# One piece of a dense product moved across two pieces of an inverse, in an order written by hand

## The chip, the core and the metric

The kernel runs on one core of a Trainium2 chip. The metric is the time of one execution on the device in microseconds (us), the median of several runs. A core has five engines, each with an instruction queue of its own that it works through in order: TensorE (PE in the profile; its loading of weights is PEld), VectorE (DVE), ScalarE (ACT), GpSimd (POOL) and SyncE (SP), which here issues the DMA transfers. An engine whose next instruction waits for a semaphore waits with all that stands behind it.

## The reference

One layer of a streaming encoder, on a sequence of 4096 tokens with 1024 features. One projection feeds four mixers of 256 features each, whose outputs are joined and projected back; a gated embedding is added and the result is normed:

```python
z = x @ w_in[i]
y_a = rwkv7_mix(rw_in, ...) * jax.nn.silu(rw_g)
y_b = pool_mix(pl_u, ...) * jax.nn.silu(pl_g)
y_c = mlstm_mix(ml_qk, ...) * jax.nn.silu(ml_g)
y_d = retention_mix(rt_q, ...) * jax.nn.silu(rt_g)
ple = jax.nn.sigmoid(x @ ple_gate[i]) * (p[i] @ ple_w[i])
x = _layer_norm(DEEPNORM_ALPHA * x + mixed @ w_out[i] + ple, ln_g[i], ln_b[i], LN_EPS)
```

The change lies in the first mixer. Per head (4 heads of 64) it carries a 64 x 64 state through the tokens, decayed, corrected by a rank-one term and read by r:

```python
def step(state, inp):
    w_t, r_t, k_t, v_t, kk_t, ab_t = inp
    sa = jnp.einsum('bhvk,bhk->bhv', state, -kk_t)
    state = (state * w_t[:, :, None, :] + sa[..., None] * ab_t[:, :, None, :]
             + v_t[..., None] * k_t[:, :, None, :])
    return state, jnp.einsum('bhvk,bhk->bhv', state, r_t)
```

## The kernel before, in words

The mixers run one after the other: pooling, retention, mLSTM, then the RWKV mixer, then the output stage. The RWKV mixer takes the sequence in 16 blocks of 256 tokens, each of four chunks of 64. Within a chunk the recurrence is solved in closed form, which needs the inverse of a triangular 64 x 64 matrix for each head and chunk (8 at a time for half a block).

The work on a block is cut into pieces, generator functions that are advanced by an order written by hand, `ORDER`. Pass i (of 18) takes the dense projections and the scores of block i, the inverse's last steps of block i - 1 and the chain over the chunks of block i - 2; in the order, `v.0` is a piece of block i, `pu.1` of block i - 1, `C` a third of a chunk of the chain. Passes 0 to 2 have orders of their own; passes 3 to 17 use `ORDER`, and a piece whose block is past the last is left out. A number behind a slash says how many steps of a piece are made. The pieces that matter here:

- `la`, `k`, `r`, `g`, `v`: dense projections (lines 158 to 160). A step is one of the eight parts of the sum over features, six matmuls of 128 x 256. After the last step the result is mixed with the token before (L1366, L1369 on ACT, L1370, L1373 on DVE, zf L1349 on POOL).
- `s0`, `s1` (L416, L417): four transposes on PE into a PSUM tile st, which DVE copies, scaled, to ST.
- `p0`, `p1` (L262 as gp, L437): sixteen score matmuls into two PSUM tiles gp, from which eight DVE instructions write g.
- `bn` (L406): a small product for the bonus term, copied by ACT.
- `inv` (L492, L496): two DMAs nd write the triangular parts of g to DRAM, four DMAs nt bring them back in another layout. `iv` (L505, L514, L530 on DVE, L532, L535 on SP) inverts 16 x 16 blocks and sends them back as X.
- `pt` (Z by a DVE transpose at L546, PE), `px` (PE, L571 on DVE): the first two products that join the blocks. `pu` (Z by a DVE transpose of X at L580, PE, copied to T by ACT at L588) and `py` (PE, L601): the last two.
- `C`: ry on PE reads the state S, ACT copies it (R, L636), sa on PE (SAV, L643), then ds on PE, S on DVE (L660), ry again and Y on ACT (L666). After the fourth chunk the output Y is normed on DVE (bsr L718, mvr L720, rsr L722, a power on POOL at L723, Y at L732 and L733), scaled (L680, L681), joined with the bonus on POOL (L677, L685) and multiplied by the gate (L686).

Tiles named st, gp, bn, vt and l share two PSUM buffers in turn: `p1`'s first gp tile takes the one that `bn` had, its second the one of `s1`.

PE's order is kept as the pieces are called. On the other engines a scheduler in the build step, with a timeline of its own, decides the order within what the data allow; the chain and the steps of the inverse are marked as urgent (`soon`). What it has decided is fixed in the program.

Of the kernel before, what the change touches and what calls it, by code (L numbers as in the profile page):

```python
# [26 lines left out]
MM = 2  # L27
WK = 2
DS = "sd"
ORDER = "C la.0 C k.0/2 C k.0 C r.0/2 C l.0 r.0/3 C n.0 r.0/4 C vt.1 r.0 m.0 C g.0/4 C g.0 v.0/2 C s0.0 v.0/1 pt.1 C p0.0 v.0/2 px.1 C bn.0 v.0/1 s1.0 v.0/2 pu.1 v.0/1 p1.0 v.0 py.1 inv.0 iv.0"  # L30

START = "v#0/3 l#0 v#0 n#0 m#0 la#1 k#1/4 bn#0 s0#0 p0#0 k#1/2 s1#0 p1#0 inv#0 k#1 r#1/2 l#1 r#1 n#1 vt#0 iv#0 m#1 g#1 v#1 bn#1 s0#1 p0#1 s1#1 p1#1 pt#0 la#2 px#0 k#2/3 pu#0 inv#1 k#2 py#0 iv#1"

# [13 lines left out]
class Trunk:  # L47
# [148 lines left out]
    def _rwkv_out(self, es):  # L196
# [493 lines left out]
        for i in range(self.NB + 2):  # L690
            gens = {}
            for w in ("" if i == 1 else START if i == 0 else THIRD if i == 2 else ORDER).split():
                if w == "C":
# [1102 lines left out]
```

## Time and profile before

| | |
|---|---|
| median of 3 runs | 2755.69 us (2754.13 to 2758.62) |
| profiled execution | 2756.33 us, of which the span from the first to the last instruction is 2754.5 us |
| mean granted TensorE clock | 0.984 of full speed |
| busy: PE, PEld | 96%, 87% of the span |
| busy: DVE, ACT, POOL | 78%, 40%, 41% |
| RWKV mixer, passes 3 to 16 | from about 1316 to 1966 us |

Times in the rows are microseconds from the start of the span. An engine's busy time counts its instructions' own spans; matmuls are pipelined, and a matmul that waits behind another in the array counts as busy too. "Idle before" an instruction is time in which its engine had nothing running, with the releaser that ended it.

### The profile page before, as it was taken

How to read it: one execution, taken by the hardware profiler on the slowest of the kernel's cores; microseconds unless marked ns; L12 is line 12 of the kernel's file. 1: busy time of each engine (PE TensorE's matmuls, PEld its weight loads, DVE VectorE, ACT ScalarE, POOL GpSimd, SP SyncE). 2: the span in 40 equal slices, each digit the busy share in tenths (PEclk: the TensorE clock that was granted, in tenths of full speed). 3: DMA queues.
4: the chain of work that ended last, by engine and by line, in shares of the span. 5: the costliest groups of instructions: out<-in, count | busy, mean ns of one | idle time of the engine just before them, and what ended most of it. 6: DMA issues, size and time to landing. Idle time of an engine off the chain costs nothing.

```text
span 2754.5 us, 57727 instructions
## 1 busy us (share of the span) xinstructions
PE 2653.0 (96%) x21940; PEld 2382.7 (87%) x21940; DVE 2142.6 (78%) x5241; ACT 1111.2 (40%) x2700; POOL 1142.9 (41%) x1302
## 2 busy tenths in 40 slices
PE   8999999998999999989999999999989999899996
PEld 8998888878899999988999999998988888778885
DVE  6767888886887777777888888888564666789997
ACT  4323222334666666653444444445222333422221
POOL 4664555554433434431323333324243111266665
PEclk9999999999999999999999999999999999999998
DMA  5453222223311112231111111113366444734431
GB/s 170 146 174 113 59 61 66 66 69 95 99 55 58 55 55 65 74 107 34 53 39 51 39 51 39 51 40 110 117 197 220 135 140 145 237 123 156 157 138 69
DMA packets 251909, 270.66 MB, mean 98 GB/s; under 512 B 69616, under 2 KB 175344, under 8 KB 251632
## 3 DMA queue, kind: packets, MB, share of 16 engines
q1 hardware_dynamic: 251632, 266.98, 31.0%
q8 instruction: 172, 2.82, 0.4%
q14 instruction: 105, 0.86, 0.1%
HBM read 203.40 MB, written 63.50 MB: 97 GB/s over the span
## 4 chain that ended last, share of the span: by engine, by line
PE 40%; DVE 16%; DMA 7%; issue 4%; POOL 3%; ACT 2%; SPq 1%; POOLq 0%; DVEq 0%; ACTq 0%
PE ry L262 2%; DVE ro L1688 2%; PE zqk L150 2%; PE zqk L151 2%; PE zqk L149 2%; DVE nt L505 1%; DVE ro L1667 1%; DVE ro L1670 1%; PE zg L158 1%; DMA nd<-g 1%; POOL ro L1671 1%; PE zg L159 1%; PE zg L160 1%; DVE so L1662 1%; PE num L1265 1%
## 5 line engine op out<-in xcount | busy, mean ns | idle before, releaser
L1446 ACT CAST Ah<-xr 128x512 fp32r<-128x512 f32 x189 | 117.0, 620 | 280.7 <-PE zrb L1482 55.3
L1447 DVE TENSOR_TENSOR Al<-xr,Ah 128x512 fp32r<-128x512 f32 x135 | 95.6, 710 | 80.6 <-ACT Ah L1446 77.2
L150 PE MATMUL zqk<-xl,wh_w_ml 128*128 128x256 f32 x512 | 150.6, 294 | 0.8 <-DVE xl L1126 0.8
L149 PE MATMUL zqk<-xh,wh_w_ml 128*128 128x256 f32 x512 | 149.8, 293 | 1.5 <-ACT xh L1125 1.2
L88 ACT CAST xh<-rawx 128x512 fp32r<-128x512 f32 x148 | 91.5, 619 | 146.4 <-DMA rawx<-in_xT 65.9
L151 PE MATMUL zqk<-xh,wl_w_ml 128*128 128x256 f32 x512 | 148.5, 290 | 0.0
L89 DVE TENSOR_TENSOR xl<-rawx,xh 128x512 fp32r<-128x512 f32 x148 | 116.0, 784 | 28.5 <-ACT xh L88 27.5
L677 POOL TENSOR_TENSOR SAV<-SAV,bon 64x256 f32<-64x256 f32 x64 | 42.9, 671 | 227.2 <-PE ry L262 226.1
L1447 POOL TENSOR_TENSOR Al<-xr,Ah 128x512 fp32r<-128x512 f32 x54 | 71.0, 1314 | 139.7 <-ACT Ah L1446 75.3
L1671 POOL TENSOR_TENSOR ro<-ro,ln_b 128x512 f32<-128x512 f32 x64 | 100.7, 1593 | 53.9 <-DVE ro L1670 53.9
L912 POOL TENSOR_TENSOR rot<-rot,sw 128x256 f32<-128x256 f32 x64 | 69.2, 1082 | 95.4 <-DVE sw L911 89.5
L149 PEld LDWEIGHTS zqk<-xh,wh_w_ml 128*128 128x128 f32 x512 | 99.1, 194 | 3.2 <-ACT xh L1125 1.5
L150 PEld LDWEIGHTS zqk<-xl,wh_w_ml 128*128 128x128 f32 x512 | 99.4, 194 | 2.9 <-DVE xl L1126 1.0
L151 PEld LDWEIGHTS zqk<-xh,wl_w_ml 128*128 128x128 f32 x512 | 99.3, 194 | 0.8
L1466 POOL TENSOR_TENSOR xr<-xr,xr 128x512 f32<-128x512 f32 x27 | 35.6, 1317 | 143.0 <-DVE xr L1463 132.7
L660 DVE SCALAR_TENSOR_TENSOR S<-ds,eC,Se 64x64 f32<-64x64 f32 x256 | 72.4, 283 | 22.0 <-PE ds L262 17.0
L1237 DVE SCALAR_TENSOR_TENSOR xc<-zc,c_convw,xc 128x256 f32<-128x256 f32 x192 | 83.3, 485 | 0.4
L437 DVE SCALAR_TENSOR_TENSOR g<-gp,rc,c_rmask 128x128 f32<-128x128 f32 x256 | 69.0, 341 | 18.3 <-PE gp L262 17.2
L149 PE MATMUL zu<-xh,wh_w_pl 128*128 128x256 f32 x256 | 74.8, 292 | 6.1 <-ACT wh_w_pl L88 6.1
L657 POOL TENSOR_TENSOR Se<-S,eC 64x128 f32<-64x128 f32 x128 | 59.2, 463 | 48.8 <-DVE S L660 44.0
L150 PE MATMUL zu<-xl,wh_w_pl 128*128 128x256 f32 x256 | 73.8, 288 | 3.9 <-DVE xl L89 3.9
L1446 ACT CAST Aho<-s 128x512 fp32r<-128x512 f32 x48 | 29.7, 621 | 115.3 <-PE zob L1482 52.4
(1130 smaller groups left out, 10570.2 us busy)
## 6 DMA issues: line engine op xcount, KB each, us to landing
rawx<-in_xT SPq DMA_DIRECT2D x148, 256.0 KB, 3.2
xr<-in_xT SPq DMA_DIRECT2D x108, 256.0 KB, 2.9
mr<-in_xT SPq DMA_DIRECT2D x64, 256.0 KB, 3.1
rp<-in_x SPq DMA_DIRECT2D x64, 256.0 KB, 3.0
s<-rp SPq DMA_DIRECT2D x64, 256.0 KB, 2.7
yo<-y SPq DMA_DIRECT2D x16, 1024.0 KB, 4.9
ro<-s SPq DMA_DIRECT2D x16, 1024.0 KB, 5.0
out<-ro SPq DMA_DIRECT2D x32, 512.0 KB, 2.6
```

The lines of the kernel that those rows point to most:

```text
L88: nc.scalar.copy(out=hi, in_=raw)
L89: eng.tensor_tensor(out=lo, in0=raw, in1=hi.bitcast(F32), op=ALU.subtract)
L149: nc.tensor.matmul(out, lh(k), rh(k), start=(k == 0 and (apart or i == 0)), stop=False, skip_group_check=True)
L150: nc.tensor.matmul(out, lh(k), rl(k), start=False, stop=False, skip_group_check=True)
L151: nc.tensor.matmul(out, ll(k), rh(k), start=False, stop=(k == nk - 1), skip_group_check=True)
L437: V.scalar_tensor_tensor(out=g1[cc][:, hh, p, e], in0=gp[hh][:, p, e], scalar=rc[:, cc, e, i:i + 1], in1=msk[:, 64 * e:64 * e + P], op0=AL ...
L660: V.scalar_tensor_tensor(out=Sn[hv, p, hv], in0=ds[hv, p], scalar=eC[hv, p, c:c + 1], in1=Se[hv, p], op0=ALU.mult, op1=ALU.add)
L912: Q.tensor_tensor(out=r3, in0=r3, in1=sw, op=ALU.add)
L1237: V.scalar_tensor_tensor(out=xc[:, t], in0=zc[t // 2][:, t % 2, j:j + TB], scalar=cw[:, t, j:j + 1], in1=xc[:, t], op0=ALU.mult, op1=ALU.add)
L1446: self.nc.scalar.copy(out=hi, in_=src)
L1447: eng.tensor_tensor(out=lo, in0=src, in1=hi.bitcast(F32), op=ALU.subtract)
L1671: Q.tensor_tensor(out=rg, in0=rg, in1=ln["ln_b", g], op=ALU.add)
```

## The change

Only the text of `ORDER` is changed, at its end:

```diff
-ORDER = "... px.1 C bn.0 v.0/1 s1.0 v.0/2 pu.1 v.0/1 p1.0 v.0 py.1 inv.0 iv.0"
+ORDER = "... px.1 C bn.0 v.0/2 s1.0 pu.1 v.0 p1.0 py.1 inv.0 iv.0"
```

Five steps of `v` come before `bn` in both. Before, one more step stands ahead of the transposes s1, and the last two between them and pu (the later mentions of `v` find it finished). Now two steps stand ahead of s1, pu follows s1 directly, and the last step of `v` stands between pu and the scores of p1.

On PE, at the end of pass 8 (z8v is the dense product of `v`, st_1 the transposes of s1, pu the step of the inverse, gp_1 the scores of p1; of the six matmuls of a step some stand outside the piece shown):

```order
-L416 MATMUL st_1_20766<-c_ident,BK_20454 128x128 x4
 L158 MATMUL z8v<-xh_6_20172,wh_w_rw_14595 128x256
 L159 MATMUL z8v<-xl_6_20171,wh_w_rw_14595 128x256
...
 L160 MATMUL z8v<-xh_6_20172,wl_w_rw_14594 128x256
+L416 MATMUL st_1_20772<-c_ident,BK_20454 128x128 x4
+L262 MATMUL pu_20780<-Z_1_20778,g_0_19733 32x32 x8
+L262 MATMUL pu_20780<-Z_1_20778,g_1_19734 32x32 x8
 L158 MATMUL z8v<-xh_6_20172,wh_w_rw_14595 128x256
...
-L262 MATMUL pu_20793<-Z_1_20791,g_0_19733 32x32 x8
-L262 MATMUL pu_20793<-Z_1_20791,g_1_19734 32x32 x8
 L262 MATMUL gp_1_0_20813<-AR_1_20456,BK_20454 128x128
```

The transposes stand one step of six matmuls later, pu one step earlier, and a step of `v` is between pu and the scores.

On DVE, the same place of the program in the kernel before (Z_1 is what pu reads, ST_1 the copy of st_1, xl_6 and xl_0 parts of coming inputs, Y the chain's output, g_1 the masked scores):

```order
L580 STREAM_TRANSPOSE Z_1_20791<-X_20145 128x512
L718 BN_STATS bsr_20718<-Y_20148 128x6 x2
L720 BN_AGGR mvr_20719<-bsr_20718 128x2 x2
L417 TENSOR_TENSOR ST_1_20472<-st_1_20766,rc_14870 128x512
L89 TENSOR_TENSOR xl_6_20911<-rawx_6_20913,xh_6_20912 128x512
...
L722 TENSOR_SCALAR rsr_20736<-mvr_20719 128x8
L732 TENSOR_TENSOR Y_20148<-Y_20148,mvr_20719 128x512
L89 TENSOR_TENSOR xl_0_21633<-rawx_0_21635,xh_0_21634 128x512
...
L1373 TENSOR_TENSOR v_20784<-v_20784,zf_20177 128x2
L437 SCALAR_TENSOR_TENSOR g_1_20474<-gp_1_0_20813,rc_14870,c_rmask 128x128 x4
L437 SCALAR_TENSOR_TENSOR g_1_20474<-gp_1_1_20814,rc_14870,c_rmask 128x128 x4
L733 TENSOR_TENSOR Y_20148<-Y_20148,rsr_20736 128x512
```

and in the changed kernel:

```order
L580 STREAM_TRANSPOSE Z_1_20778<-X_20145 128x512
L718 BN_STATS bsr_20718<-Y_20148 128x6 x2
L89 TENSOR_TENSOR xl_6_20911<-rawx_6_20913,xh_6_20912 128x512
L720 BN_AGGR mvr_20719<-bsr_20718 128x2 x2
L417 TENSOR_TENSOR ST_1_20472<-st_1_20772,rc_14870 128x512
L722 TENSOR_SCALAR rsr_20736<-mvr_20719 128x8
L732 TENSOR_TENSOR Y_20148<-Y_20148,mvr_20719 128x512
...
L437 SCALAR_TENSOR_TENSOR g_1_20474<-gp_1_0_20813,rc_14870,c_rmask 128x128
...
L1373 TENSOR_TENSOR v_20806<-v_20806,zf_20177 128x2
L733 TENSOR_TENSOR Y_20148<-Y_20148,rsr_20736 128x512
L437 SCALAR_TENSOR_TENSOR g_1_20474<-gp_1_0_20813,rc_14870,c_rmask 128x128 x3
L437 SCALAR_TENSOR_TENSOR g_1_20474<-gp_1_1_20814,rc_14870,c_rmask 128x128 x4
```

ST_1 now stands behind xl_6 and a second pair of mvr, and L733 before seven of the eight g. Passes 3 to 6 and 8 to 13 are moved alike. A little later, where the inverse of the block begins, one instruction changes sides in these passes:

```order
 L309 TENSOR_TENSOR lal_18103<-la_17985,lah_18102 64x256
+L686 SCALAR_TENSOR_TENSOR Y_17188<-Y_17188,sg_16084 128x512
 L505 TENSOR_TENSOR nt_17894<-nt_17894,xs_14868 64x4
-L686 SCALAR_TENSOR_TENSOR Y_17188<-Y_17188,sg_16084 128x512
 L514 TENSOR_REDUCE xs_14868<-nt_17894 64x4
```

The gate product of Y stands before the inverse's first product instead of behind it. In pass 7 the scheduler has set another order on DVE, here from Z_1 on in the changed kernel:

```order
L580 STREAM_TRANSPOSE Z_1_20038<-X_19405 128x512
L718 BN_STATS bsr_19978<-Y_19408 128x6 x4
L720 BN_AGGR mvr_19979<-bsr_19978 128x2 x4
L722 TENSOR_SCALAR rsr_19996<-mvr_19979 128x8
L732 TENSOR_TENSOR Y_19408<-Y_19408,mvr_19979 128x512
L89 TENSOR_TENSOR xl_6_20171<-rawx_6_20173,xh_6_20172 128x512
L733 TENSOR_TENSOR Y_19408<-Y_19408,rsr_19996 128x512
L680 TENSOR_TENSOR Y_19408<-Y_19408,c_rw_ln_w 128x512
L417 TENSOR_TENSOR ST_1_19732<-st_1_20032,rc_14871 128x512
L681 TENSOR_TENSOR Y_19408<-Y_19408,c_rw_ln_b 128x512
```

In the kernel before, pass 7 has the same order as pass 8; here ST_1 stands behind L732, L733 and L680.

## Rows read from the trace of the kernel before

**Rows 1.** The page, busy time of each engine

```profile
PE 2653.0 (96%) x21940; PEld 2382.7 (87%) x21940; DVE 2142.6 (78%) x5241; ACT 1111.2 (40%) x2700; POOL 1142.9 (41%) x1302
```

**Rows 2.** Timeline of PE, pu: start, length, engine, line, out<-in, count [idle before]

```profile
1543.21 0.69 PE L262 MATMUL pu<-Z,g 32*32 32x32 f32 x32
...
1587.92 0.69 PE L262 MATMUL pu<-Z,g 32*32 32x32 f32 x32
...
1861.76 0.69 PE L262 MATMUL pu<-Z,g 32*32 32x32 f32 x32
```

**Rows 3.** Timeline of PE, the chain's third ry, passes 8 and 9

```profile
1566.67 0.62 PE L262 MATMUL ry<-S,AR 128*128 128x128 f32 x4
...
1611.81 1.10 PE L262 MATMUL ry<-S,AR 128*128 128x128 f32 x4 [0.26 <-DVE S L660]
```

**Rows 4.** Timeline of DVE, the start of the inverse after pass 8

```profile
1601.42 0.16 DVE L505 TENSOR_TENSOR nt<-nt,xs 64x4 f32<-64x4 f32 x1 [1.22 <-DMA nt<-nd]
1601.51 0.68 DVE L686 SCALAR_TENSOR_TENSOR Y<-Y,sg 128x512 f32<-128x512 f32 x1
1602.11 0.15 DVE L514 TENSOR_REDUCE xs<-nt 64x4 f32<-64x4 f32 x1
```

**Rows 5.** Timeline of SP, issues of nd and nt after passes 7 and 8

```profile
1548.85 1.26 SPq L492 DMA_DIRECT2D nd<-g  x2
1551.87 1.81 SPq L496 DMA_DIRECT2D nt<-nd  x4
...
1593.55 1.26 SPq L492 DMA_DIRECT2D nd<-g  x2
1598.17 1.81 SPq L496 DMA_DIRECT2D nt<-nd  x4
```

**Rows 6.** Timeline of PE, two neighbouring dense matmuls of pass 8

```profile
1587.59 0.28 PE L159 MATMUL z8v<-xl,wh_w_rw 128*128 128x256 f32 x1
1587.71 0.28 PE L160 MATMUL z8v<-xh,wl_w_rw 128*128 128x256 f32 x1
```

**Rows 7.** Timeline of DVE, from Z to g in pass 8

```profile
1587.06 0.69 DVE L580 STREAM_TRANSPOSE Z<-X 128x512 f32<-128x512 f32 x1
...
1588.17 0.69 DVE L417 TENSOR_TENSOR ST<-st,rc 128x512 f32<-128x512 f32 x1
1588.77 0.68 DVE L89 TENSOR_TENSOR xl<-rawx,xh 128x512 fp32r<-128x512 f32 x1
1589.37 0.24 DVE L720 BATCH_NORM_AGGREGATE mvr<-bsr 128x2 f32<-128x6 f32 x2
1589.53 0.45 DVE L1370 SCALAR_TENSOR_TENSOR v<-z8v,c_prm,v 128x255 f32<-128x255 f32 x1
1589.90 0.16 DVE L722 TENSOR_SCALAR rsr<-mvr 128x8 f32<-128x8 f32 x1
...
1591.63 2.15 DVE L437 SCALAR_TENSOR_TENSOR g<-gp,rc,c_rmask 128x128 f32<-128x128 f32 x8
```

**Rows 8.** Timeline of PE, the scores p1 of pass 8 and p0 of pass 9

```profile
1588.55 1.52 PE L262 MATMUL gp<-AR,BK 64*128 64x128 f32 x16
...
1626.14 1.16 PE L262 MATMUL gp<-AR,BK 64*128 64x128 f32 x16
```

**Rows 9.** Timeline of POOL and DVE, the power and who waits for it

```profile
334.10 2.62 POOL L723 TENSOR_TENSOR rst<-rst,pw 128x8 f32<-128x8 f32 x1
336.75 1.77 DVE L733 TENSOR_TENSOR Yt<-Yt,rst 128x512 f32<-128x512 f32 x1 [0.22 <-POOL rst L723]
...
1545.43 2.01 POOL L723 TENSOR_TENSOR rsr<-rsr,pw 128x8 f32<-128x8 f32 x1 [1.60 <-DVE rsr L722]
...
1590.13 2.63 POOL L723 TENSOR_TENSOR rsr<-rsr,pw 128x8 f32<-128x8 f32 x1 [1.59 <-DVE rsr L722]
```

**Rows 10.** PE in pass 15, then stretches: busy PE, PEld, DVE, ACT, POOL, granted clock, DMA

```profile
1884.09 1.03 PE L262 MATMUL n<-ones,sq 128*64 128x2 f32 x16 [1.37 <-ACT sq L340]
...
1881.00:1885.00 4.00, 2.51 (x40) 2.15 (x38) 4.00 (x9) 3.63 (x9) 1.94 (x2) 1.00 0.57 182
1885.30:1888.70 3.40, 3.40 (x18) 3.40 (x18) 3.29 (x11) 1.26 (x2) 1.26 (x4) 0.50 0.30 77
```

More of the change, by code (lines that the diff above doesn't have):

```diff
@@ L29 @@
 DS = "sd"
-ORDER = "C la.0 C k.0/2 C k.0 C r.0/2 C l.0 r.0/3 C n.0 r.0/4 C vt.1 r.0 m.0 C g.0/4 C g.0 v.0/2 C s0.0 v.0/1 pt.1 C p0.0 v.0/2 px.1 C bn.0 v.0/1 s1.0 v.0/2 pu.1 v.0/1 p1.0 v.0 py.1 inv.0 iv.0"
+ORDER = "C la.0 C k.0/2 C k.0 C r.0/2 C l.0 r.0/3 C n.0 r.0/4 C vt.1 r.0 m.0 C g.0/4 C g.0 v.0/2 C s0.0 v.0/1 pt.1 C p0.0 v.0/2 px.1 C bn.0 v.0/2 s1.0 pu.1 v.0 p1.0 py.1 inv.0 iv.0"
 START = "v#0/3 l#0 v#0 n#0 m#0 la#1 k#1/4 bn#0 s0#0 p0#0 k#1/2 s1#0 p1#0 inv#0 k#1 r#1/2 l#1 r#1 n#1 vt#0 iv#0 m#1 g#1 v#1 bn#1 s0#1 p0#1 s1#1 p1#1 pt#0 la#2 px#0 k#2/3 pu#0 inv#1 k#2 py#0 iv#1"
```

## The prediction

> **What bounds the kernel now.** The page's summary comes first: TensorE (PE) is busy 96% of the span [rows 1]. Taken alone that says that PE is the bound and that every wait added to PE is paid in full. The timeline of PE says it more finely. The second product of the inverse (pu) stands once in every pass, so its starts give the pace: from pass 8 to pass 14 it is (1861.76 - 1587.92) / 6 = 45.64 us, while pass 7 takes 1587.92 - 1543.21 = 44.71 us, 0.93 less [rows 2]. I compared the instructions of the two group by group: PE takes the same time for all of them, to 0.1 us, except at one place. There the step of the recurrence (ry, reading the state S) follows the dense matmuls without a pause in the short pass; in the normal one PE idles 0.26 us for DVE's S (L660), and the four matmuls then take 1.10 us instead of 0.62 [rows 3]: with the dense pipeline running empty before them, from start to start the 0.9 us. So about 0.9 us of PE's "busy" in each normal pass is waiting, and the pace is set by a second loop: VectorE's (DVE's) masked scores g of p1, their transfer to DRAM (nd) and back (nt), the row sums of the inverse (L505, L514, L530) on DVE, then S on DVE, then PE. The list of waits confirms its DMA part: DVE waits for nt in 11 of the passes, 1.22 us in pass 8 [rows 4]. In the short pass the second nd issue to the first nt issue takes 1551.87 - 1548.85 = 3.0 us, in a normal one 1598.17 - 1593.55 = 4.6 us [rows 5]. PE alone would do a pass in 44.7; the loop through DVE and DMA makes it 45.6. A change is worth what it does to the later of these two.
>
> **The change part by part.** It exists in 13 passes (3 to 15; in 16 and 17 the pieces v, s1 and p1 have no block left). No instruction is added or removed; the order fences show what moves. I work on pass 8 and then count.
>
> *PE, pu earlier.* Six dense matmuls, 0.12 us apart [rows 6], leave the place before pu: 0.72 us. In before pu starts at 1587.92 just behind them; without them it could at 1587.20. But pu reads Z, which DVE ends only at 1587.06 + 0.69 = 1587.75 [rows 7], and what DVE does before Z is not moved. So PE now waits some 0.55 us for Z, and starts pu hardly earlier (0.1 us) with 0.7 us of dense work still to do. In before, this piece of v was what covered Z.
>
> *PE, the second scores.* The scores gp of p1 need the PSUM buffer that the transposes st hold until DVE has copied them (ST, L417): before, gp takes 1.52 us here and 1.16 us at the first scores, where nothing is waited for, so 0.36 us is already that wait [rows 8]. On DVE, ST now stands behind xl_6 and two of the mvr: it moves by 1589.53 - 1588.77 = 0.76 us [rows 7]. gp's release moves with it, from 1588.86 to 1589.62, and the moved dense piece (1587.8 + 0.6 for pu + 0.8 = 1589.2) hides beneath. PE leaves this place 0.76 us later than before. PE's own pace becomes 44.71 + 0.76 = 45.47 us, still below 45.64: in a normal pass this alone costs nothing, since the 0.9 us wait for S shrinks by as much. Where that cover is gone (pass 7) it costs in full.
>
> *DVE, the scores g.* Y's second factor (L733) stood behind g and now stands before seven of its eight instructions. All else ahead of g is the same set, so DVE comes to L733 at g's old start 1591.63 plus one g (2.15 / 8 = 0.27), 1591.9. L733 reads the power that GpSimd (POOL) forms: in pass 8 it starts 0.23 us after rsr's start and takes 2.63 us; in pass 7 2.01 us [rows 9]. rsr moves to 1588.17 + 0.76 + 0.60 = 1589.53; the small zf on POOL may stand in front, so the power starts at about 1589.9 and ends at 1591.9 or 1592.5. DVE waits 0 or 0.6 us for it, L733 takes 0.60 (start to start, as xl does, 1589.37 - 1588.77 [rows 7]), and g ends 0.6 or 1.2 us later. nd and nt follow g, so nt lands that much later; DVE was waiting for it already.
>
> *DVE, the gate product.* L686 stood inside the inverse, behind its first L505, and now stands before it, in the time in which DVE waits for nt. The chain from nt to S loses it: 1602.11 - 1601.51 = 0.60 us [rows 4]. This is the change's one gain on the loop. Net on S: 0.6 - 0.6 = 0, with hand-overs say +0.1, or 1.2 - 0.6 = +0.6, say +0.7. Of the ten normal passes (3 to 6 and 8 to 13) five show the short power and five the long: 10 x 0.4 = 4.0 us, with 0 and 7 as bounds (all short, all long).
>
> Whether POOL's span may be trusted decides half of this. The row: in the retention stage the power starts at 334.10 and ends, by its 2.62 us, at 336.72; DVE, idle and waiting for it, starts at 336.75 [rows 9]. The Trainium skill (Perfetto Trace Analysis, Per-instruction lifecycle) tells readers to treat a GpSimd span in a profile as unreliable and to go by the spacing of instructions. By that rule the long powers need not be longer, and the term would be 10 x 0.1 = 1 us, the whole sum 7.5 instead of 10.5. Here the spacing agrees with the span, so I keep 4.0.
>
> *Pass 7.* There the new order on DVE is another: Z, all eight small statistics, rsr, Y, xl_6, L733, L680 and only then ST. With pass 8's durations: Z starts 0.27 earlier (1586.79), rsr is due at 1588.3, the power (2.01) ends at 1590.6, then L733 and L680 at 0.7 each, so ST starts at 1592.0 instead of 1588.17. gp, and all PE work behind it, moves by 3.8 us, and pass 7 is the one without a wait for S to take it up: +3.8 (with a long power +4.4). During such a wait the granted clock may fall: in pass 15, shortly after PE had idled 1.37 us for sq, the granted clock of 1885.3 to 1888.7 is 0.50, the lower of the two levels, 1.2 GHz, and 1.00 before [rows 10]. At half clock 3.4 us of dense work loses 1.7 us: +1.7, bounds 0 and two such stretches, 3.4.
>
> *Passes 14 and 15.* Gate weights and the first products of the last stage are mixed in, and DVE has hardly a pause. g ends 0.6 to 1.8 us later, part of it taken up by waits for weights. I take +0.5 each, bounds -0.3 and +1.2.
>
> **Sum:** 4.0 + 3.8 + 1.7 + 1.0 = 10.5 us on the profiled execution's 2756.33, giving 2766.8; that execution lies 0.64 above the median 2755.69, so 2766.2 for a median, +0.38%. The bounds: 0 + 3.8 + 0 - 0.6 = +3.2 and 7 + 4.4 + 3.4 + 2.4 = +17.2.
>
> **Rivals.**
> 1. *Absorbed.* The loop gains from L686 as much as it loses by g in every pass, or nd takes 3.0 us instead of 4.6 at its new place. In the second case PE's 45.47 is the pace: 10 x -0.17 = -1.7; with pass 7 at 3.8 and the rest at 0.5 to 1 the sum is 3 us: 2758.5, no change that can be told (0.2% is 5.5 us). For it: two passes show 3.0 us without any edit; against it: they are 2 of 12, with nd and the work around it placed as in the others.
> 2. *Heavier.* All powers long, the clock falls twice, and pass 7 also meets the 4.6 us nd (+1.6 there and in pass 14): 7 + 4.4 + 3.4 + 3.2 = 18: 2773.5. For it: the long power stood in a row in passes 8 to 10. Against: it needs several at once.
> 3. *Faster.* The loop through nd is the bound, and it is the one freed: nd at 3.0 us in all passes, while PE's new wait turns out under 0.2 us, because gp's first matmul has its buffer and ST is taken no later than now. Then the pace goes to 44.9: 10 x (44.9 - 45.64) = -7.4 or 2748. It decides where nd is under 3.6 us and the gp wait does not grow. Against it: ST's place on DVE is fixed by the program, and the row of gp already shows that PE waits for it.
>
> **How the numbers follow.** Forecast 0.48, absorbed 0.24, heavier 0.20, faster 0.08. Slower by over 0.2% (5.5 us, what a measurement of this kernel can tell): all of heavier and nine tenths of the forecast, 0.64 with rounding; within 0.2%: the absorbed case and the forecast's low end, 0.27; faster 0.09. The forecast's own range is 2760 to 2772; 8 in 10 with the others, 2757 to 2775.
>
> **What would show it.** Right: pu waiting for Z (L580) about 0.55 us in every changed pass; gp of p1 still released by ST, PE there 0.76 us later; in half the passes DVE L733 idle "until POOL rsr"; nt's first L505 still waiting, with L514 straight behind it; ry's wait for S left at 0.2 to 0.9 us; a pace of 45.7 to 46.3; pass 7 longer by 4 us or more, all of it at gp. Wrong: a pace of 45.5 or less (nd near 3.0 us: rival 1, or 3 if PE does not wait at gp); pass 7 within 1 us of the others; pu starting before 1587.7's equivalent, which would mean that Z is not what holds it.

## The result and the profile after

The changed kernel takes 2772.14 us (median of 7 runs, 2765.28 to 2778.94) against 2758.62 us for the kernel before (7 runs). The ratio on record is 1.0053, with a 95% interval of 1.004 to 1.0066; the two medians alone give 1.0049. It is slower by 13.5 us where 10.5 were forecast; 2772.14 lies 0.14 above the forecast's own range (2760 to 2772) and inside the wider one (2757 to 2775). The profiled execution took 2772.91 us; its span is 2771.0 us (before 2754.5), 16.5 us more. All ratios here leave out executions in a slow state of the chip, of which there was one: 3612.05 us, in run 8 below.

The starts of pu split this up. A "normal" pass is one of 3 to 6 and 8 to 13.

| part | before | after | more | forecast |
|---|---|---|---|---|
| 10 normal passes, mean | 45.645 | 46.045 | 10 x 0.40 = 4.0 | 4.0 |
| pass 7 | 44.71 | 51.55 | 6.8 | 3.8 + 1.7 |
| passes 14 and 15 | 104.61 | 108.60 | 4.0 | 1.0 |
| up to pu of pass 3 | 1360.59 | 1361.92 | 1.3 | 0 |
| behind pu of pass 16 | 788.1 | 788.5 | 0.4 | 0 |

The first and the last stretch differ by more than this among the kernels below that repeat no matmuls (1357.7 to 1365.5 us and 782.3 to 789.1 us), so nothing is read from their 1.3 and 0.4.

Before, PE's timeline had no wait at pu and pass 7 was the short one [rows 2]. After, in the same view (start, length, engine, line, out<-in, count, idle before and its releaser), passes 7 and 9:

```profile
1545.53 0.69 PE L262 MATMUL pu<-Z,g 32*32 32x32 f32 x32 [0.33 <-DVE bsr L718]
...
1547.06 0.49 PE L262 MATMUL gp<-AR,BK 64*128 64x128 f32 x2
1550.68 2.07 PE L262 MATMUL gp<-AR,BK 64*128 64x128 f32 x14 [3.13 <-DVE ST L417]
...
1643.16 0.69 PE L262 MATMUL pu<-Z,g 32*32 32x32 f32 x32 [0.63 <-DVE bsr L718]
...
1644.69 1.37 PE L262 MATMUL gp<-AR,BK 64*128 64x128 f32 x16
...
1667.52 1.10 PE L262 MATMUL ry<-S,AR 128*128 128x128 f32 x4
```

PE now waits 0.63 us in front of pu. The releaser that the view names, L718, is the instruction behind Z on DVE; Z itself ends 0.15 us before pu starts. In pass 7 PE waits 3.13 us in the middle of gp, for ST. And ry still takes 1.10 us: PE is still late for S, as before [rows 3].

DVE in pass 9, from Z to the start of the inverse (the answer to [rows 7] and [rows 4]):

```profile
1642.32 0.69 DVE L580 STREAM_TRANSPOSE Z<-X 128x512 f32<-128x512 f32 x1
...
1644.16 0.69 DVE L417 TENSOR_TENSOR ST<-st,rc 128x512 f32<-128x512 f32 x1
...
1646.49 0.34 DVE L437 SCALAR_TENSOR_TENSOR g<-gp,rc,c_rmask 128x128 f32<-128x128 f32 x1
...
1647.22 0.69 DVE L733 TENSOR_TENSOR Y<-Y,rsr 128x512 f32<-128x512 f32 x1
1647.84 1.89 DVE L437 SCALAR_TENSOR_TENSOR g<-gp,rc,c_rmask 128x128 f32<-128x128 f32 x7
...
1655.34 0.68 DVE L686 SCALAR_TENSOR_TENSOR Y<-Y,sg 128x512 f32<-128x512 f32 x1
1657.32 0.16 DVE L505 TENSOR_TENSOR nt<-nt,xs 64x4 f32<-64x4 f32 x1 [1.31 <-DMA nt<-nd]
1657.52 0.15 DVE L514 TENSOR_REDUCE xs<-nt 64x4 f32<-64x4 f32 x1
```

g ends 6.57 us behind pu's start, before 5.86: 0.71 later, which is L733 (0.62 from start to start). L514 follows L505 at 0.20 us where it took 0.69 with L686 between them [rows 4]. POOL's power, which I had put at 2.0 or 2.6 us [rows 9], takes 1.64 us and ends at 1647.19, just before L733 starts at 1647.22; POOL's row of the same pass:

```profile
1645.55 1.64 POOL L723 TENSOR_TENSOR rsr<-rsr,pw 128x8 f32<-128x8 f32 x1
```

In nine of the ten normal passes L733 starts 0.03 us behind the power's end, the same distance as in passes 7 and 15, where it waits for the power visibly. So it comes just in time: it starts 0.09 us behind the start of the small instruction ahead of it (L1373), a wait of a few hundredths at most. With the 2.0 or 2.6 us of before it would have waited some 0.4 or 1.0 us (my estimate from these rows).

Pass 7 on DVE, and the stretches behind it (busy time and instructions of PE, PEld, DVE, ACT, POOL, then the granted clock, DMA share and GB/s):

```profile
1548.48 0.69 DVE L733 TENSOR_TENSOR Y<-Y,rsr 128x512 f32<-128x512 f32 x1 [0.93 <-POOL rsr L723]
1549.21 0.69 DVE L680 TENSOR_TENSOR Y<-Y,c_rw_ln_w 128x512 f32<-128x512 f32 x1
1549.93 0.69 DVE L417 TENSOR_TENSOR ST<-st,rc 128x512 f32<-128x512 f32 x1
```

```profile
1545.50:1548.00 2.50, 2.02 (x40) 1.68 (x40) 2.02 (x10) 1.56 (x5) 1.64 (x2) 1.00 0.03 9
1551.00:1554.00 3.00, 3.00 (x47) 2.71 (x46) 3.00 (x9) 0.69 (x2) 2.49 (x3) 0.50 0.11 21
1554.00:1557.00 3.00, 3.00 (x16) 3.00 (x16) 1.84 (x6) 0.88 (x3) 0.72 (x1) 0.53 0.30 96
1557.00:1560.00 3.00, 3.00 (x42) 2.79 (x42) 0.55 (x2) 0.99 (x4) 0.00 (x0) 1.00 0.50 125
```

ST stands behind a wait for POOL, L733 and L680. From the end of PE's 3.13 us pause the granted clock is at 0.50, the lower level, until shortly before 1557 (0.53 is the mean of the third stretch), and then back at 1.00.

Over passes 3 to 13 the list of waits shows the same in sums (engine, instruction and what it waited for: us in total, times, longest). PE before, then PE after:

```profile
PE ry L262 <- DVE S L660: 2.0, 8, 0.3
```

```profile
PE pu L262 <- DVE bsr L718: 6.0, 11, 0.6
PE gp L262 <- DVE ST L417: 3.1, 1, 3.1
PE ry L262 <- DVE S L660: 0.4, 2, 0.2
```

### The profile page after: what moved, and what is told of

The parts are those of the page before. It is cut to its first block, busy times and chain, and to the rows that moved or that the text cites. A ratio compares the mean times of both kernels' runs of the same rounds, so it can differ in the third digit from the quotient of the medians.

```text
span 2771.0 us, 57722 instructions
## 1 busy us (share of the span) xinstructions
PE 2656.9 (96%) x21940; PEld 2385.6 (86%) x21940; DVE 2148.2 (78%) x5241; ACT 1110.2 (40%) x2700; POOL 1146.8 (41%) x1302
## 3 DMA queue, kind: packets, MB, share of 16 engines
q8 instruction: 172, 2.82, 0.4%
## 4 chain that ended last, share of the span: by engine, by line
PE 39%; DVE 18%; DMA 7%; issue 4%; POOL 3%; ACT 2%; SPq 1%; POOLq 0%; DVEq 0%; ACTq 0%
DVE ro L1688 2%; PE zqk L150 2%; PE zqk L151 2%; PE zqk L149 2%; PE ry L262 2%; DVE nt L505 2%; DVE ro L1667 1%; DMA nd<-g 1%; DVE ro L1670 1%; DVE g L437 1%; PE zg L158 1%; POOL ro L1671 1%; PE zg L159 1%; PE zg L160 1%; DVE so L1662 1%
## 5 line engine op out<-in xcount | busy, mean ns | idle before, releaser
L88 ACT CAST xh<-rawx 128x512 fp32r<-128x512 f32 x148 | 91.5, 619 | 147.3 <-DMA rawx<-in_xT 71.5
## 6 DMA issues: line engine op xcount, KB each, us to landing
out<-ro SPq DMA_DIRECT2D x32, 512.0 KB, 2.6
```

The lines of the kernel that those rows point to most:

```text
L88: nc.scalar.copy(out=hi, in_=raw)
```

## The experiments

The profile after offers two places for the loss: PE's new wait for Z (6.0 us in the list) and the later scores on DVE. My theory was the second. All runs were timed in five rounds beside the kernel before; "3 to 13" is the time from pu of pass 3 to pu of pass 14 in the profiled execution, "14, 15" the two passes behind.

| run | ratio to before (95%) | 3 to 13 | 14, 15 |
|---|---|---|---|
| before | 1 | 501.2 | 104.6 |
| the change | 1.0053 (1.004 to 1.0066) | 512.0 | 108.6 |
| 1: s1 later only | 1.0038 (1.0023 to 1.0053) | 510.4 | 108.1 |
| 2: pu earlier only | 0.9992 (0.9983 to 1.0002) | 497.6 | 106.8 |
| 3: change, ST first | 1.0025 (1.0016 to 1.0033) | 505.6 | 107.2 |
| 4: change, ST and g first | 1.0003 (0.9992 to 1.0013) | 499.3 | 108.6 |
| 5: before, fetch moved | 1.0073 (1.0061 to 1.0085) | 497.2 | 104.8 |
| 6: change, fetch moved | 1.0107 (1.0094 to 1.012) | 500.7 | 109.3 |
| 7: run 4, fetch moved | 1.0031 (1.002 to 1.0042) | 500.5 | 110.1 |
| 8: before, v behind g | 0.9983 (0.9973 to 0.9994) | 495.2 | 106.9 |
| 9: before, L686 ahead | 0.9955 (0.9943 to 0.9966) | 492.6 | 104.7 |
| 10: run 8, L686 late | 0.9968 (0.9955 to 0.998) | 491.7 | 107.7 |

**1 and 2: the two halves of the change.** Each alone; the rest of `ORDER` is that of the kernel before.

```diff
-bn.0 v.0/1 s1.0 v.0/2 pu.1 v.0/1 p1.0 v.0 py.1
+bn.0 v.0/2 s1.0 v.0/1 pu.1 v.0/1 p1.0 v.0 py.1   (run 1)
+bn.0 v.0/1 s1.0 v.0/1 pu.1 v.0 p1.0 py.1         (run 2)
```

> Only the transposes s1 are moved one step of v later; pu stays behind all of v. On DVE this gives the changed kernel's order (ST behind xl_6 and the second pair of mvr; L733 before seven of the g; in pass 7 ST behind L732, L733 and L680). Theory 'ST and the scores' (the loss comes from where ST and L733 stand on DVE): pu does not wait for Z, gp waits longer for ST, g ends 0.7 us later, pace 46.1 us in the normal passes, pass 7 about 51.5: 14 to 17 us over the kernel before, ratio 1.005 to 1.006. Rival 'pu waits for Z' (the loss is the 0.63 us that PE waits in each pass before pu): no wait there, pace 45.6, only pass 7 longer, 6 to 8 us, ratio 1.002 to 1.003.

> Only pu is moved one step of v earlier; the transposes s1 stay where they were in the kernel before. On DVE the order is that of the kernel before but for v (L1370, L1373), which now stands behind the scores g. Theory 'ST and the scores': PE waits 0.6 us for Z, but ST is copied while the last step of v runs, so gp does not wait (0.36 us less), and g ends about 0.4 us earlier because v is behind it; pace 45.2 to 45.4, no long pass: 2 to 5 us under the kernel before, ratio 0.998 to 0.999. Rival 'pu waits for Z': pace 46.1 as in the changed kernel, 5 to 8 us over the kernel before, ratio 1.002 to 1.003.

Run 1 loses 9.2 us in passes 3 to 13 without any wait at pu; pass 7 takes 51.53 us, and PE waits there as in the changed kernel:

```profile
1545.61 0.69 PE L262 MATMUL pu<-Z,g 32*32 32x32 f32 x32
1546.23 0.48 PE L262 MATMUL gp<-AR,BK 64*128 64x128 f32 x2
1550.45 1.43 PE L262 MATMUL gp<-AR,BK 64*128 64x128 f32 x14 [3.73 <-DVE ST L417]
```

Run 2 has the wait for Z in every pass and is not slower. gp takes 1.16 us, the length without a wait that [rows 8] show for p0:

```profile
1583.89 0.69 PE L262 MATMUL pu<-Z,g 32*32 32x32 f32 x32 [0.64 <-DVE bsr L718]
1585.42 1.16 PE L262 MATMUL gp<-AR,BK 64*128 64x128 f32 x16
```

So the loss goes with s1, and "pu waits for Z" falls as its cause: that wait is 0.64 us in a kernel whose pace is 45.23. It is not free, though: every pass of run 2 takes 45.1 to 45.3 us with hardly a wait for nt (at most 0.15 us), so PE's own pace there is 45.23 instead of 44.71, and it is hidden only because the kernel before went at 45.64. My expectation for run 1 was a little high (1.005 to 1.006, a pace of 46.1): its ten normal passes take 45.89 in the mean, and nd, which will matter below, was slow in three of them only.

**3 and 4: the new order on PE with other orders on DVE.** Both are the changed kernel, with ST, or ST and the scores g, at high priority.

```diff
+            with self.soon():
+                V.tensor_tensor(out=bl[b]["ST"][cc]...      (runs 3 and 4, L417)
...
+            with self.soon():
+                for hh in range(2):                           (run 4, L437)
...
+                            V.scalar_tensor_tensor(out=g1[cc]...
```

> The changed kernel with ST (L417) at high priority. Pass 7 then has the same order on DVE as the other passes (ST ahead of rsr and L732); in all of them ST stands one mvr earlier and L733 before three of the g instead of seven. Theory 'ST and the scores': pass 7 takes 45.4 to 46.2 instead of 51.55, its granted clock stays at 1.00, the others stay at 46.0 (L733 still before the end of g): 5 to 6.5 us under the changed kernel, 8 to 10 over the kernel before, ratio 1.003 to 1.004. Rival 'pu waits for Z' expects pass 7 at 46.1 too and the other passes unchanged, so this run does not part them; a rival in which the long pass 7 is due to something else (the granted clock by itself) expects it to stay at about 51.

> The changed kernel's order of pieces on PE with ST and the scores g (L417, L437) both at high priority: L733 stands behind all of g again, the gate product L686 inside the inverse again, pass 7 like the others. It is the new order on PE with nearly the old one on DVE. Theory 'ST and the scores': g ends 5.9 to 6.0 us after pu instead of 6.57 (5.86 before), the loop takes 45.6 to 45.8, PE alone 45.4: pace 45.7, pass 7 45.4 to 45.7; 2 to 4 us over the kernel before, ratio 1.0005 to 1.0015. Rival 'pu waits for Z': the pace stays at 46.1, 9 to 11 us over, ratio 1.003 to 1.004.

Run 3: pass 7 takes 45.95 us, PE does not pause in gp, and the pass is now like the others, which stay at 45.96 in the mean. The ratio, 1.0025, is a little under the expected 1.003 to 1.004. Run 4 takes L733 behind g and L686 back into the inverse, and the whole loss of passes 3 to 13 is gone: its pace is 45.39, below the kernel before. The order on PE therefore costs nothing there against the pace of before; what the scheduler made of it on DVE does. But 45.39 is less than the 45.7 I expected, though g ends 6.04 us behind pu, later than before (5.86). DVE hardly waits for nt (at most 0.08 us, in pass 10 0.47); pass 8:

```profile
1593.98 0.68 DVE L733 TENSOR_TENSOR Y<-Y,rsr 128x512 f32<-128x512 f32 x1
...
1600.39 0.15 DVE L505 TENSOR_TENSOR nt<-nt,xs 64x4 f32<-64x4 f32 x1
1600.46 0.68 DVE L686 SCALAR_TENSOR_TENSOR Y<-Y,sg 128x512 f32<-128x512 f32 x1
```

This made the length of nd the next question. There are two kinds of passes. The DMA view of the changed kernel (queue q8; then out<-in, issues, KB, median us from issue to landing), first of pass 5, the one normal pass with the pace of run 4 (45.44), then of pass 9, whose last line is the range for the single issues:

```profile
q8 instruction: 1, 0.02, 1.3%
nd<-g SPq DMA_DIRECT2D x2, 64.0 KB, 2.1
nt<-nd SPq DMA_DIRECT2D x3, 16.0 KB, 1.9
...
q8 instruction: 1, 0.02, 1.7%
nd<-g SPq DMA_DIRECT2D x2, 64.0 KB, 3.0
...
DMA to landing us min/median/max: 2.1/3.0/3.8
```

The 3.0 is thus the middle of two issues: the first nd lands in 2.1 us as ever, the second in 3.8. Over the passes 3 to 14 of all twelve kernels the slower nd takes 3.1 to 4.0 us or, in the other kind of pass, 2.1 to 2.3.

A packet of queue q8 lies beside nd in both, but not at the same moment: its packet time stamp is 2.04 us behind the last nd issue in pass 5 and 1.56 in pass 9. The page counts 172 such packets with 2.82 MB, 16 KB each; over the 43,880 matmuls and weight loads of PE that makes 64 bytes each, so I took them for PE's instructions. A pass has about 1,270 of these, and five packets fall at nearly the same places in each.

**5, 6 and 7: moving the fetch.** One line repeats the small matmuls of bn for block 0, so that all later instructions stand elsewhere in their packets (117, 116 and 6 more; shown for 117).

```diff
-                        mm(bn[64 * e:64 * e + 64, cc, 2 * p:2 * p + 2], ...
+                        for _ in range(1 + (14 + (4 * cc + 2 * e + p < 5) if b == 0 else 0)): mm(bn[...
```

> The kernel before, with 117 of the small matmuls of bn repeated once for block 0 only, ahead of the repeated passes (they write the same values again, some 4 us of PE at the start). Order in the passes as before. Theory 'instruction fetch': PE's instructions come in packets of 16 KB (queue q8, about 1 us on one DMA engine), five in a pass of about 1,280 instructions, so at the same places in every pass; in the kernel before one starts 1.1 to 1.9 us after the last nd issue and holds one nd packet up, by which nt comes 1.3 us later. 117 matmuls more, 234 instructions of 256, put every later fetch about 11 matmuls later, 1.2 us, behind nd: DVE no longer waits for nt, pace 44.7 us in all passes from 3 to 13 instead of 45.64, 9 us less, minus the 4 us of the repeated matmuls: ratio 0.997 to 0.999. Rival 'nd to nt takes this long by itself' (its length depends on when g ends, or on the other transfers): pace stays at 45.6, the time 4 us over the kernel before, ratio 1.0015.

> The changed kernel with 116 of the small matmuls of bn repeated for block 0. Through them the scheduler also gives pass 7 the order of the other passes on DVE. Theory 'instruction fetch': the fetch moves from 1.2 to 1.6 us behind the last nd issue to about 2.6, nt comes 1.3 us earlier, and the pace is PE's own, 45.4 us, in all passes from 3 to 13, as in the one pass (5) of the changed kernel that had no collision: 13 to 14 us under the changed kernel for pass 7 and the pace, 4 us back for the repeated matmuls: 2760 to 2763, ratio to the kernel before 1.001 to 1.003. Rival: the pace stays at 46.1 and only pass 7 is mended: ratio 1.004 to 1.005.

> The kernel of the fourth run (ST and the scores at high priority in the changed order), with 6 of the small matmuls of bn repeated for block 0, 0.2 us of PE. Theory 'instruction fetch': it moves the fetch 6 matmuls, 0.7 us, earlier, from 1.7 to 1.9 us behind the last nd issue (no collision) to 1.0 to 1.2 (collision); nt comes 1.3 us later, DVE waits for it 0.7 to 0.9 us in the passes, pace 45.7 to 46.0 instead of 45.38: 3 to 6 us over the fourth run, ratio to the kernel before 1.0015 to 1.0025. Rival 'nd to nt takes this long by itself': the pace stays at 45.38 and the ratio at 1.0003.

I had miscounted the instructions: one such matmul has two records and two weight loads, so 117 are 468 (174 packets instead of 172, as the page says; 468 times 64 bytes are 1.8 packets of 16 KB). Yet the packets moved about as meant: in run 5 they come 2.3 to 3.0 us behind the last nd issue (before 1.1 to 1.9), in run 7 0.6 to 1.7 in passes 3 to 8. Passes 5 and 9 of run 7, the same kernel with the packet 0.62 and 1.96 us behind:

```profile
nd<-g SPq DMA_DIRECT2D x2, 64.0 KB, 3.3
nt<-nd SPq DMA_DIRECT2D x1, 16.0 KB, 1.6
...
nd<-g SPq DMA_DIRECT2D x2, 64.0 KB, 2.1
nt<-nd SPq DMA_DIRECT2D x3, 16.0 KB, 1.9
```

In passes 3 to 8 of run 7 nd takes 2.7 to 3.5 us (median of the two), in 9 to 13 it takes 2.1; in runs 5 and 6 it takes 2.1 in all passes from 3 to 13. In run 5, pass 4, nd has the short time, but the packet now meets nt (2.4, where it is 1.9 in the changed kernel's pass 5 above):

```profile
nd<-g SPq DMA_DIRECT2D x2, 64.0 KB, 2.1
nt<-nd SPq DMA_DIRECT2D x2, 16.0 KB, 2.4
```

So the theory holds in kind and was too large in size: run 5 gains 4.0 us over passes 3 to 13, not 9; run 6 gains 11.3 over the changed kernel, of which 6.1 are pass 7 in its other order, with a pace of 45.4 to 45.7; run 7 loses 1.2 against run 4, not 3 to 6, because most of the wait for nt (0.4 to 1.1 us) is taken up before PE needs S. Run 7 also answers a doubt about run 4, which differs from the changed kernel in DVE's order and, by where the packets fell, in nd: with nd slow, passes 3 to 8 of run 7 still take 45.58 in the mean, 0.5 under the changed kernel's slow passes (46.11). So DVE's order is the larger part of what run 4 gave back. All three totals are spoilt by the added matmuls: in run 5 pu of pass 1 starts at 1304.98 instead of 1275.83, 29 us later where I had expected 4 (see the last section).

**8, 9 and 10: shortening the loop.** Run 8 puts the mixing of v behind g, run 9 puts L686 ahead of the inverse, run 10 adds to run 8 that L686 goes behind the S that follows the inverse.

```diff
+            if nm == "v" and b > 2: yield 0.1                       (run 8)
+            with tc.issue_after(state["g", b, 1].ins) ...:
+                self.mixed(b, t, z, 2 * g, 2)
...
-            V.scalar_tensor_tensor(out=Y, in0=Y, scalar=0.5, ...    (run 9)
+            state['gate'] = V.scalar_tensor_tensor(out=Y, ...
...
+            with self.soon(), (tc.issue_after(state["gate"].ins) ...: (run 9, around iv)
...
+                if c == 1 and "late" in state:                      (run 10)
+                    with tc.issue_after(sl.ins):
+                        state.pop("late")()
```

> The kernel before with its order on PE in the passes, but the mixing of v (L1370, L1373) queued on DVE behind the scores g of p1 instead of ahead of them (one more yield in v's step, and its mixing issued behind g; the gate product L686 then also falls one place further into the inverse). Theory 'loop and instruction fetch': g ends 0.85 us earlier, nd is issued about 5.5 us after pu, the fetch at 7.5 to 8.2 then comes 2.0 us or more behind it and meets nothing, nt lands 2 us earlier, S is no longer late and the pace is PE's own, 44.7 us, from pass 3 to 13: 8 to 10 us under the kernel before, ratio 0.9963 to 0.9973. Rival 'the pace is PE's own already' (its 0.9 us at ry has another cause than nt): pace 45.6, ratio 1.000.

> The kernel before with one thing of the changed kernel alone: on DVE the gate product L686 queued ahead of the inverse's first product L505 (in the time in which DVE waits for nt), in passes 2 to 15. PE and all else as before. Theory 'loop': S comes 0.5 us earlier after nt, PE's wait at ry falls from 0.9 to 0.4, pace 45.15 instead of 45.64: 4 to 5 us under the kernel before, ratio 0.998 to 0.9987. Rival 'the pace is PE's own': pace 45.6, ratio 1.000. If nt also lands at another time against the fetch, its wait changes with it: passes without a collision go at 44.7.

> The kernel of the eighth run (v mixed behind the scores g) with the gate product L686 and its store moved out of the inverse, behind the second S of the next chain; the last reduction of the inverse then stands ahead of that S. In the eighth run PE still waited 0.27 us at ry for S, with L686 (0.6 us) inside the inverse and the last reduction (0.33 us) behind S. Theory 'loop': S comes 0.27 us earlier, just in time: the pace is PE's own 44.7 in passes 3 to 13 against 45.03: 3 to 3.5 us under the eighth run, ratio to the kernel before 0.9965 to 0.9975. Rival: S stays late because DVE has no pause left there, pace 45.0, ratio 0.998.

Run 8: DVE hardly waits for nt any more (at most 0.24 us), but L686 still stands between the inverse's first product and S. S starts 22.6 us behind pu instead of 23.3, and the pace falls by about as much, to 45.03, not to 44.7. Run 10 takes L686 out: S starts at 22.0, and the pace is 44.70, PE's own. Run 9 is the best kernel, 0.45% faster than before, more than the 0.2% I expected of L686. Its rows show why for passes 3 to 13 (DVE in pass 8; the last two lines are the same place in the kernel before):

```profile
1597.61 0.68 DVE L686 SCALAR_TENSOR_TENSOR Y<-Y,sg 128x512 f32<-128x512 f32 x1
1598.59 0.16 DVE L505 TENSOR_TENSOR nt<-nt,xs 64x4 f32<-64x4 f32 x1 [0.30 <-DMA nt<-nd]
...
1607.09 1.20 DVE L660 SCALAR_TENSOR_TENSOR S<-ds,eC,Se 64x64 f32<-64x64 f32 x4
1608.32 0.60 DVE L505 TENSOR_TENSOR nt<-xs,nt 64x256 f32<-64x256 f32 x1
...
1610.67 0.57 DVE L505 TENSOR_TENSOR nt<-xs,nt 64x256 f32<-64x256 f32 x1
1611.17 1.20 DVE L660 SCALAR_TENSOR_TENSOR S<-ds,eC,Se 64x64 f32<-64x64 f32 x4
```

In the kernel before the last product of the inverse stands ahead of S, and S starts 9.75 us behind the first L505 [rows 4]; here S goes first and starts 8.50 us behind. So run 9 did not change one thing alone, as I had written: the scheduler also set S ahead of a product. With 1.25 us gained PE no longer waits at ry (0.61 us for its four matmuls, as in [rows 3]'s short pass):

```profile
1608.88 0.61 PE L262 MATMUL ry<-S,AR 128*128 128x128 f32 x4
```

It does so although nd is slow in eight of its passes 3 to 13: with the rest of the loop shorter, a late nt costs little here (44.80 in the mean). Passes 3 to 13 are 8.6 of the 12.7 us by which its profiled span is shorter; 5.3 more lie behind pu of pass 16, where the mean granted clock is 0.98 instead of 0.97 (26 us at the lower level instead of 43). That L686 has a part in those is not shown.

## Why the prediction was right, and where not

The direction and the mechanism came out: 10.5 us were forecast, 13.5 measured between the medians. Of the parts one fitted by luck and two were too small.

*The loop through DVE and DMA bounds the normal passes.* Shown: runs 8 to 10 leave PE's order in passes 3 to 13 as it was and bring the normal passes from 45.645 to 45.03, 44.80 and 44.70, where the prediction put PE alone at 44.71. One reading in it is off without harm: 3.0 and 4.6 us are counted from the start of the first of the two nd issues that [rows 5] merge, not of the second. From the second issue it is 2.34 and 3.93 us; the difference, 1.6 us, is the same.

*PE alone comes to 45.47 with the new order.* Shown: run 4 goes at 45.39, pass 5 of the changed kernel at 45.44, with hardly a wait for nt. pu waits 0.63 us where 0.55 was forecast, ST ends 0.75 us later against 0.76. The terms were shared out wrongly, though: the prediction gave all of it to ST and let the moved piece of v hide beneath, but run 2, in which ST is not later, already goes at 45.23. Some 0.5 us of the 0.7 comes with pu's new place, the rest with ST.

*g ends 0.6 or 1.2 us later, L686 gives 0.6 back.* The 0.4 of a normal pass came out (46.045 - 45.645), but by other terms, and that was luck. The long power that half the passes were to wait for did not exist: it takes 1.64 us in the normal passes, and L733 comes just as it ends. What failed is the step that took POOL's durations of before into the changed kernel. g ends 0.71 later in all ten; L505 starts 0.8 later in the nine passes in which nd is slow. L686 gives 0.48 to 0.49 back, not 0.60, and most of that is lost again before S. In seven of these nine passes the inverse's last product ahead of S takes 0.95 to 0.97 us, where it takes 0.57 to 0.59 in nine of the ten normal passes before; pass 9, after:

```profile
1665.98 0.96 DVE L505 TENSOR_TENSOR nt<-xs,nt 64x256 f32<-64x256 f32 x1
```

What lengthens it was not tested. From the first L505 to S it is therefore only 0.27 us less (9.51 instead of 9.78 in the mean of the nine), S starts 0.53 later, and these passes lose 0.47. Pass 5, where the packet of q8 missed nd, gained 0.2, and that makes the mean 0.40.

The Trainium skill (Perfetto Trace Analysis, Per-instruction lifecycle) tells readers to treat a GpSimd span in a profile as unreliable. Here the spans agreed with DVE's waits in both traces, in pass 7 to 0.03 us; the mistake was not to trust a span but to carry it over.

*Pass 7.* The mechanism was right in every part, the sizes small: forecast 3.8 for ST's place and 1.7 for the clock, 5.5; measured 6.84. ST ends 5.09 us behind pu's start instead of 0.94, +4.15. The other 2.7 are PE's work behind the pause, while the granted clock is at its lower level: from ST's end to py it takes 2.06 us instead of 1.14, +0.9, and py, ry and the 24 dense matmuls of la then take 0.99 + 0.87 + 4.05 = 5.9 us instead of 4.1, +1.8. Run 3 confirms the cause by taking it away.

*Passes 14 and 15.* Mis-sized: 4.0 us for 1.0. The term knew of waits, but not that they let the clock fall here too. In pass 14 (+2.2) PE is idle for 4.6 us instead of 3.3. In pass 15 (+1.8) PE waits in one piece for R, which stands on ACT behind casts of weights (L88) that wait for their DMA. The rows are PE before, PE after, ACT after, and a stretch after with the columns as above:

```profile
1925.22 0.50 PE L262 MATMUL sa<-R,X 64*64 64x64 f32 x5 [0.53 <-ACT R L636]
...
1940.99 0.80 PE L262 MATMUL sa<-R,X 64*64 64x64 f32 x5 [3.47 <-ACT R L636]
...
1937.42 1.32 ACT L88 CAST wpwhg<-rawwple 128x512 fp32r<-128x512 f32 x2 [1.21 <-DMA rawwple<-in_w_ple]
...
1939.20:1945.90 6.70, 4.91 (x44) 4.04 (x45) 5.52 (x18) 4.08 (x9) 3.87 (x4) 0.50 0.49 128
```

PE's 4.9 busy us at half clock cost some 2.5 us (an estimate from this row); in the kernel before the granted clock is 1.00 through all of pass 15. The other runs agree: before and runs 5 and 9, with 104.6 to 104.8 us, wait 0.5 us there and keep the clock; runs 2, 3, 4, 6, 7, 8 and 10, with 106.8 to 110.1, wait 2.4 to 5.3 us for R, and it falls. Runs 8 and 10 have PE's order of before in passes 3 to 13 and still the long wait, so the places of s1 and pu alone do not decide it; why R is late in one kernel and not in another stays open, and run 1 (108.1) has its loss without that wait.

*Rival "absorbed".* It rested on nd at its short time. That does occur, and run 4, which also has no long pass 7, is what it would look like: 1.0003. In the changed kernel it happened in one of ten passes only. Whether the packet of q8 hits is a matter of a few tenths of a us, which the trace of before could not tell for a new order.

## What to carry to other kernels

A reordering on one engine is also a reordering by the scheduler on the others; compare the order of every engine first, since here the same order on PE cost 0.5% or nothing that could be told, and in passes 3 to 13 the difference was mostly DVE's order. Find the loop that sets the pace by comparing an odd short pass with the normal ones, and then remove instructions from that loop, not from the busiest engine. Pin what stands before a transfer or between a transfer and its consumer, and do not carry a GpSimd duration over to a new neighbourhood.

## What the runs showed of the hardware

- A 16 KB packet of queue q8 (by the count above, PE's instructions) beside the two nd lengthened one of them, in two passes both, from 2.1 us to between 3.1 and 4.0. Over passes 3 to 14 of all twelve kernels, 144 in all, this happened in each of the 40 passes in which the packet's time stamp lay 0.62 to 1.56 us behind the last nd issue, and in none of the 70 in which it lay 1.93 us or more behind. Between 1.68 and 1.92 it happened in 7 of 34, so the moment alone does not decide there.
- The power on POOL took 1.64 us in the normal passes after, as in those of runs 2 (but for one) and 4, and 2.0 or 2.6 before, on the same 128x8 elements; the cause was not looked for.
- In the changed kernel the granted clock fell from 1.00 to 0.50 during PE's pauses of 3.1 us (pass 7) and 3.5 us (pass 15), and the matmuls behind them ran slowly for some 5 us; in pass 15 of the kernel before, with no pause over 1.4 us, it stayed at 1.00.
- The repeated small matmuls of run 5, with the 16 records that they repeat, took 22.9 us, most of the 29. The rows (PE, start to end of the window; columns as above) show PE busy throughout, at the lower level of the clock:

```profile
1235.00:1245.00 10.00, 10.00 (x100) 10.00 (x100) 0.00 (x0) 0.00 (x0) 0.00 (x0) 0.50 0.01 2
```

There one of 250 records takes 0.09 us, two and a half times the 0.037 us of the 16 records in the kernel before (0.59 us). The clock's factor of two explains most of it; the rest is open.
